# First weights on ScalarE's queue, rounded by VectorE; x, the norm's factors and y in one tile; the first step product by product

## The chip, the cores and the metric

The kernel runs on one core of one Trainium2 chip. The metric is the device time of one execution in microseconds. The time before is the median of three executions, 852.4 us (852.05 to 853.03).

A core has a matrix engine (TensorE, PE in the profile, its weight loads PEld), a vector engine (VectorE, DVE), a scalar engine (ScalarE, ACT), a third elementwise engine (GpSimd, POOL) and an engine that only issues transfers here (SyncE, SP). SP and ACT can both issue transfers (SPq and ACTq in the profile). PE accumulates into PSUM banks; ACT, DVE and POOL work on SBUF tiles of 128 partitions.

## The reference

Two encoder layers over 512 tokens of 1024 features. Each layer is RMS norm, one wide input projection, a local attention, a SiLU gate, an output projection and a residual sum:

```python
def rms_norm(x, g):
    xf = x.astype(jnp.float32)
    y = xf * lax.rsqrt(jnp.mean(xf * xf, axis=-1, keepdims=True) + RMS_EPS)
    return (y * g.astype(jnp.float32)).astype(x.dtype)

def mixer_a(hn, w_in, w_out, q_gain, k_gain, t5_bias):
    proj = hn @ w_in                       # 1024 x (9 * 1024 + 1024)
    for g, (window, dilation) in enumerate(DILATED_PAIRS):
        q = rms_norm(qkv[:, :, g, 0], q_gain[g])
        k = rms_norm(qkv[:, :, g, 1], k_gain[g])
        o, lse = dilated_group_attention(q, k, qkv[:, :, g, 2], ...)
        ...
    y = jnp.sum(alpha[..., None] * jnp.stack(outs), axis=0)
    return (y.reshape(b, s, BRANCH_WIDTH) * jax.nn.silu(gate)) @ w_out

def reference(x, norm_gain, ...):
    for i in range(DEPTH):                 # DEPTH = 2
        hn = rms_norm(x, norm_gain[i])
        y = mixer_a(hn, ...) if i % 2 == 0 else mixer_b(hn, ...)
        x = x + y
    return x
```

The second mixer has the same form with attention on an 8 x 64 grid of tokens. Everything is float32.

## The kernel before, in words

**Products.** The matrix engine takes float32 operands in a rounded form (F32R). To keep float32 precision each operand is split in a rounded part h and the rest l, and each product is made of three matmuls into one bank: h by h, h by l, l by h (`mm3`). Weights are loaded as plain float32 (`wraw`), and `split` makes `wh` (rounding copy on ScalarE, line 127) and `wl` (the difference, line 131, on VectorE or, for two of five, on GpSimd). The same is done with the normed input: `norm` makes `hn_h` (ScalarE, line 379) and `hn_l` (VectorE, line 380) from x and the norm's factors `ng`. The row scale of the norm is not in `hn`; it is multiplied in after the projection.

**Steps.** A projection (`project`) adds over eight steps k of 128 features. In each step four blocks of 128 tokens get one product (three matmuls) each, so a step is twelve matmuls of 128 x 512. The order on PE is the order of the program; the instructions of the other engines are placed by a scheduler with a model of time, except those under `keep_in_program_order`, which stay where they stand. A second thread of the program (`side`) emits norms, squares and attention between the matmuls: after each block of matmuls the main thread lets it go on as far as a modelled clock says.

**Streams.** `raws` loads the weights in the order of use, two steps in one tile of 1024 columns (`wraw`, three buffers), all on SP's queue. The first tile is loaded in two halves, with x's second slice between them. `splits` works up to four steps ahead (four buffers of `wh` and `wl`).

**The start.** SP issues x's first slice (128 x 512), the first weights (128 x 512), x's second slice, the second weights, and then larger pieces of x and weights in turn. ScalarE's queue issues `ng` (128 x 16) and `hg` (128 x 8, the head gains). VectorE makes four products `gk` of `hg` (line 366); first use is much later, in `k_a`. Meanwhile PE runs nine matmuls on ones (`busy`, line 358) whose result is not used. Then step 0 begins. `side` squares each slice of x in place once it is normed (`square_a`), adds the slices up (line 1146) and gets the row scale.

**y.** x's first copy `x_all` (16 KB per partition) has the tag "y"; when it is no longer read, `y_h` takes its place. `y_l` is a tile of its own. Both are written once per head pair (`put_y`) and read by the output projections (`out_product`).

Of the kernel before, what the change touches and what calls it, by code (L numbers as in the profile page):

```python
# [13 lines left out]
F32 = mybir.dt.float32  # L14
F32R = mybir.dt.float32r
I32 = mybir.dt.int32
AF = mybir.ActivationFunctionType
ALU = mybir.AluOpType
# [4 lines left out]
P = 128  # L23
S = 512
# [3 lines left out]
KT = 8  # L28
EPS = 1e-6
SCALE = DH ** -0.5  # L30
# [12 lines left out]
def tile_hybrid_encoder(  # L43
# [2 lines left out]
    xt: bass.AP,  # L46
    xg: bass.AP,
    w: bass.AP,
    norm_gain: bass.AP,
    head_gain: bass.AP,  # L50
    t5t: bass.AP,
    rpb: bass.AP,
# [4 lines left out]
    nc = tc.nc  # L57
# [3 lines left out]
    big = ctx.enter_context(tc.tile_pool(name="big", bufs=1))  # L61
# [21 lines left out]
    def bank(name):  # L83

        return ps_side.tile([P, 512], F32, tag="side", name=name)
# [13 lines left out]

    hn_h = big.tile([P, KT, S], F32R, name="hn_h")  # L100
    hn_l = big.tile([P, KT, S], F32R, name="hn_l")
    x_all = big.tile([P, KT, S], F32, tag="y", name="x_all")
    y_l = big.tile([P, KT, S], F32R, name="y_l")

    def rsqrt(eng, r, ss, n, scale):
        v = wk.tile([P, 32], F32, tag="nv", name="nv", bufs=1)
# [15 lines left out]
    turn, pool = [0], [2, 5]  # L122

    def split(raw, n):
        h = wp.tile([P, 512], F32R, tag="wh", name="wh", bufs=4)[:, :n]
        l = wp.tile([P, 512], F32R, tag="wl", name="wl", bufs=4)[:, :n]
        nc.scalar.copy(h, raw)  # L127
        turn[0] += 1
        to_pool = turn[0] * pool[0] % pool[1] < pool[0]
        eng = nc.gpsimd if to_pool else nc.vector  # L130
        eng.tensor_sub(l, raw, h.bitcast(F32))  # L131
        return h, l
# [24 lines left out]
    def loads():  # L157
        for off, n, ks in blocks():
            per = 1024 // n
            for k in range(0, ks, per):  # L160
                m = min(per, ks - k)
                yield w[:, off + k * n : off + (k + m) * n], m * n, n
# [3 lines left out]
    def raws():  # L166
        queue = []
        for src, cols, n in loads():
            raw = wp.tile([P, 1024], F32, tag="wraw", name="wraw", bufs=3)
            dst = raw[:, :cols]  # L170
            if not begun:
                nc.sync.dma_start(dst[:, :n], src[:, :n])
                begun.append(load_x(1, 2))
                dst, src = dst[:, n:], src[:, n:]
            nc.sync.dma_start(dst, src)
            if behind:
                behind.pop()()
            queue.append((raw, cols, n))
            if len(queue) > 2:
                yield queue.pop(0)  # L180
        yield from queue
# [30 lines left out]
    def mm3(o, lh, ll, rh, rl, first, last):  # L212
        matmul(o, lh, rh, start=first, stop=False)
        matmul(o, lh, rl, start=False, stop=False)
        matmul(o, ll, rh, start=False, stop=last)
# [26 lines left out]
    def project(stat_h, stat_l, n, evac, guard, need=None):  # L242

        acc = {i: ps_acc.tile([P, 512], F32, tag="acc", name="acc") for i in range(4)}
        for k in range(KT):
            chore(1 <= k < KT - 2)
            if need:
                yield need, min(k + 1, KT - 1)
            if k == KT - 1:
                yield guard  # L250
            h, l = next(wsteps)
            for i in range(4):
                mm3(acc[i][:, :n], stat_h(k, i), stat_l(k, i), h, l, k == 0, k == KT - 1)
                if k == KT - 1:
                    evac(i, acc[i])
                yield
# [69 lines left out]
    ng = cp.tile([P, 2, KT], F32, name="ng")  # L326
# [13 lines left out]
        rsqrt(nc.vector, rs_n, ssq, 4, 1.0 / D)  # L340

    def load_x(k0, k1):
        nc.sync.dma_start(x_all[:, k0:k1, :], xt[:, k0:k1, :])

    warm = cp.tile([P, 1], F32, name="warm")
    nc.vector.memset(warm, 0.0)
    nc.scalar.activation(warm, warm, AF.Exp)
    load_x(0, 1)
    nc.scalar.dma_start(ng, norm_gain)
    behind += [  # L350
        lambda: load_x(6, KT),
        lambda: load_x(4, 6),
        lambda: load_x(2, 4),
    ]
    busy = bank("busy")
    for _ in range(9):
        wide = lambda n: ones[:, 0:1].to_broadcast([P, n])
        nc.tensor.matmul(busy, wide(P), wide(S), start=True, stop=True)
    wsteps = steps()
    wsteps = chain([next(wsteps)], wsteps)  # L360

    hg = cp.tile([P, 8], F32, name="hg")
    nc.scalar.dma_start(hg, head_gain)
    gk = cp.tile([P, 4], F32, name="gk")
    for i, (a, b) in enumerate(((0, 3), (1, 4), (2, 5), (6, 7))):
        nc.vector.scalar_tensor_tensor(
            gk[:, i : i + 1], hg[:, a : a + 1], -SCALE, hg[:, b : b + 1], op0=ALU.mult, op1=ALU.mult
        )

    def scales_a():  # L370
        pa = spread()
# [2 lines left out]

    def norm(layer, k, xk):

        g = ng[:, layer, k : k + 1]
        h, l = hn_h[:, k, :], hn_l[:, k, :]
        nc.scalar.activation(h, xk, AF.Copy, scale=g)
        return nc.vector.scalar_tensor_tensor(l, xk, g, h.bitcast(F32), op0=ALU.mult, op1=ALU.subtract)  # L380
# [38 lines left out]
    st = {}  # L419
# [237 lines left out]
    def put_y(hc, o, permuted, last):  # L657

        gt, rest = st.pop(("gate", hc))
        for _ in rest:  # L660
            pass
        if last and permuted:
            for c in range(4):
                q = slice(P * c, P * c + P)
                of = lambda t: t.rearrange("p (s x) -> p s x", x=16)[:, :, 4 * c : 4 * c + 4]
                nc.vector.tensor_mul(of(gt), of(gt), of(o))
                src = gt.rearrange("p (t ja x) -> p x ja t", t=4, ja=8)[:, 4 * c : 4 * c + 4]
                h, l = (t[:, hc, q].rearrange("p (x ja t) -> p x ja t", x=4, ja=8) for t in (st["y_h"], y_l))
                nc.scalar.copy(h, src)
                nc.vector.tensor_sub(l, src, h.bitcast(F32))  # L670
            return
        h, l, src = st["y_h"][:, hc, :], y_l[:, hc, :], gt
        if permuted:

            tc.keep_in_program_order(nc.vector.tensor_mul(gt, gt, o))
            src = gt.rearrange("p (t ja x) -> p x ja t", t=4, ja=8)
            h, l = (t.rearrange("p (x ja t) -> p x ja t", t=4, ja=8) for t in (h, l))
        else:
            for grid, line in ((mid_rc, mid_o), (edge_rc, edge_o)):
                nc.vector.tensor_mul(grid(gt), grid(gt), line(o))  # L680
        nc.scalar.copy(h, src)
        (nc.vector if last else nc.gpsimd).tensor_sub(l, src, h.bitcast(F32))
        stamp["ya" if permuted else "yb", hc, "y"] = 0
# [239 lines left out]
    def out_product(key, sink):  # L923


        acc = {}

        def step(k, tiles):
            h, l = next(wsteps)
            for i, f in enumerate(tiles):  # L930
                c = slice(P * i, P * i + P)
                mm3(acc[f], h[:, c], l[:, c], st["y_h"][:, k, :], y_l[:, k, :], k == 0, k == KT - 1)
                if k == KT - 1:
                    sink(f, acc[f])
                yield

        for f in range(4):
            acc[f] = ps_acc.tile([P, 512], F32, tag="acc", name="acc")
        for k in range(KT - 1):
            chore(True)  # L940
            yield key, k, "y"
            yield from step(k, range(4))
        yield key, "turned"
        for f in range(4, 7):
            acc[f] = bank("acc2")
        for k in range(KT - 1):
            yield from step(k, range(4, 7))
        yield key, KT - 1, "y"
        yield from step(KT - 1, range(4))
        yield from step(KT - 1, range(4, 7))  # L950
        acc[7] = ps_acc.tile([P, 512], F32, tag="acc", name="acc")
        for k in range(KT):
            yield from step(k, (7,))
# [182 lines left out]
    def side():  # L1136
        for k in range(KT):
            norm(0, k, x_all[:, k, :])
            if k:
                square_a(k - 1)  # L1140
            stamp["na", k] = 0
            yield 1000
        square_a(KT - 1)
        for k in range(1, KT):
# [1 line left out]
            nc.vector.tensor_add(x_all[:, 0, :], x_all[:, 0, :], x_all[:, k, :])  # L1146
        yield 1500
        row_scale(row_sums(x_all[:, 0, :]))
        st["y_h"] = big.tile([P, KT, S], F32R, tag="y", name="y_h")
        yield 2500  # L1150
        bias_lines()
        st["e", 0] = bias_a(0)
# [64 lines left out]
def _layout(x, norm_gain, a_w_in, a_w_out, a_q_gain, a_k_gain, t5_bias,  # L1217
            b_w_in, b_w_out, b_q_gain, b_k_gain, b_rpb):
    f = lambda a: np.asarray(a)
    x, norm_gain, t5_bias = f(x), f(norm_gain), f(t5_bias)  # L1220
# [13 lines left out]
    for hc in range(NHC):  # L1234
        c = lambda g, i: (3 * g + i) * D + P * hc
# [9 lines left out]
    w = np.concatenate(parts, axis=1)  # L1245

    hg = np.concatenate([f(a_q_gain)[0], f(a_k_gain)[0], f(b_q_gain), f(b_k_gain)]).T
    hg = np.concatenate([hg, hg])
    rt = f(b_rpb)[0].transpose(0, 2, 1)
    rpb = np.stack([rt[:, :, 7 - r + _GRID_ROWS] for r in _GRID_ROWS], axis=1).reshape(P, 248)  # L1250
    oh, mask = _constants()
    norm_gain = norm_gain.reshape(2, KT, P).transpose(2, 0, 1)
    xt = x[0].reshape(P, 4, KT, P).transpose(3, 2, 1, 0).reshape(P, KT, S)
    xg = x[0].reshape(8, 64, KT, P)[_GRID_ROWS].transpose(3, 2, 1, 0).reshape(P, KT, S)
    return [xt, xg, w, norm_gain, hg, t5_bias.T, rpb, oh, mask]


_NAMES = ["xt", "xg", "w", "norm_gain", "head_gain", "t5t", "rpb", "onehot", "maskc"]


# [17 lines left out]
```

## Time and profile before

| | before |
|---|---|
| median of the runs | 852.4 us |
| the profiled execution's own time | 854.65 us |
| span of that execution in the profile | 852.7 us |
| TensorE busy | 843.6 us (99%) |
| VectorE, ScalarE, GpSimd busy | 520.2, 431.3, 307.1 us |
| transfers | 141.23 MB, mean 166 GB/s |

The span runs from the first to the last instruction; the execution's own time is longer by what lies around it. A row of the timeline gives the start and the duration in us, the engine, the line of the kernel, the operation, what is written from what, the shape, and in brackets how long the engine had been idle before and what ended that. Matmuls are pipelined and their ends are modelled, so the distance of two starts says more of PE's pace than a duration. A row of the waits gives engine, line and tile, what it waited for, and us in total, number, longest. In a row of windows stand the window, its length, the busy time and number of instructions of PE, PEld, DVE, ACT and POOL, the granted clock, the DMA engines' busy share, and GB/s.

### The profile page before, as it was taken

What the parts mean: (1) busy time and instruction counts of PE and PEld (TensorE: products, weight loads), DVE (VectorE), ACT (ScalarE), POOL (GpSimd) and SP (SyncE); (2) the same over time, 40 slices, a digit from 0 to 9 for tenths busy, and PEclk for the clock granted to TensorE, in tenths of its full rate; (3) what the DMA queues carried; (4) which work ended last, traced back from release to release, by engine and by line L of the source; (5) the groups of instructions that cost most, each with busy time, mean ns of one, the idle gap of its engine ahead of it and who ended that gap; (6) DMA issues with size and microseconds to landing.
All of it is one profiled execution on the core that took longest, in us unless ns stands there. A gap on an engine that the chain in (4) does not pass through costs nothing.

```text
span 852.7 us, 15400 instructions
## 1 busy us (share of the span) xinstructions
PE 843.6 (99%) x5547; PEld 702.7 (82%) x5547; DVE 520.2 (61%) x1335; ACT 431.3 (51%) x924; POOL 307.1 (36%) x493
## 2 busy tenths in 40 slices
PE   8999999999999999999999999999999999999998
PEld 6788878788788788788788787789998898889786
DVE  6445684674675675675675745447567656766642
ACT  7433653653652652652653554355366655665531
POOL 2252541542542542542531341121344335542411
PEclk9999999999999999999999999999999999999999
DMA  7346277477478378378375562174245654555223
GB/s 250 111 130 208 87 226 219 153 222 227 137 230 241 105 239 240 98 238 238 96 247 153 147 190 78 60 244 142 82 142 150 168 162 149 170 163 160 99 98 126
DMA packets 65372, 141.23 MB, mean 166 GB/s; under 512 B 5904, under 2 KB 23248, under 8 KB 65296
## 3 DMA queue, kind: packets, MB, share of 16 engines
q1 hardware_dynamic: 65008, 140.24, 53.7%
q8 instruction: 44, 0.72, 0.4%
q14 instruction: 32, 0.26, 0.1%
q10 hardware_dynamic: 288, 0.01, 0.0%
HBM read 109.11 MB, written 31.12 MB: 164 GB/s over the span
## 4 chain that ended last, share of the span: by engine, by line
PE 87%; ACT 4%; DMA 4%; DVE 3%; issue 1%; POOL 1%; SPq 0%; ACTq 0%; POOLq 0%; DVEq 0%
PE acc L206 74%; PE log L206 5%; PE o L206 5%; PE tp L210 3%; DMA qd<-rawq 1%; ACT p L655 1%; ACT p L814 1%; DMA rp<-in_rpb 1%; ACT p L1067 1%; DMA qt<-qd 1%; POOL sq L270 1%; ACT wh L127 1%; DMA hg<-in_head_gain 0%; DVE wl L131 0%; DMA eb<-lb_d 0%
## 5 line engine op out<-in xcount | busy, mean ns | idle before, releaser
L127 ACT CAST wh<-wraw 128x512 fp32r<-128x512 f32 (+1 forms) x276 | 162.0, 588 | 291.4 <-PE acc L206 251.0
L206 PE MATMUL acc<-wh,hn_h 128*128 128x512 f32 (+1 forms) x768 | 294.2, 383 | 1.7 <-ACT wh L127 0.9
L206 PE MATMUL acc<-wh,hn_l 128*128 128x512 f32 (+1 forms) x768 | 286.3, 373 | 0.0
L206 PE MATMUL acc<-wl,hn_h 128*128 128x512 f32 (+1 forms) x768 | 285.8, 372 | 0.4 <-DVE wl L131 0.4
L131 POOL TENSOR_TENSOR wl<-wraw,wh 128x512 fp32r<-128x512 f32 (+1 forms) x110 | 137.0, 1245 | 359.4 <-ACT wh L127 320.0
L131 DVE TENSOR_TENSOR wl<-wraw,wh 128x512 fp32r<-128x512 f32 (+1 forms) x166 | 111.1, 670 | 135.8 <-ACT wh L127 131.5
L206 PEld LDWEIGHTS acc<-wh,hn_h 128*128 128x128 f32 x768 | 144.6, 188 | 29.3 <-issue 4.9
L206 PEld LDWEIGHTS acc<-wh,hn_l 128*128 128x128 f32 x768 | 144.4, 188 | 20.8
L206 PEld LDWEIGHTS acc<-wl,hn_h 128*128 128x128 f32 x768 | 144.8, 189 | 19.8 <-DVE wl L131 0.9
L206 PE MATMUL acc<-hn_h,wh 128*128 128x512 f32 x192 | 77.0, 401 | 0.9 <-ACT rawq L460 0.6
L206 PE MATMUL acc<-hn_h,wl 128*128 128x512 f32 x192 | 74.9, 390 | 0.0
L206 PE MATMUL acc<-hn_l,wh 128*128 128x512 f32 x192 | 74.8, 390 | 0.0
L655 ACT ACTIVATE p<-p,mn 128x512 f32<-128x512 f32 (+3 forms) x128 | 69.3, 586 | 0.0
L814 ACT ACTIVATE p<-p,mn 128x512 f32<-128x512 f32 (+1 forms) x64 | 44.8, 701 | 45.0 <-DVE mn L803 44.1
L273 DVE TENSOR_REDUCE ss<-sq 128x4 f32<-128x256 f32 (+1 forms) x96 | 48.4, 504 | 30.7 <-POOL sq L272 19.7
L727 DVE STREAM_TRANSPOSE tr<-p 128x512 f32<-128x512 f32 (+1 forms) x80 | 53.7, 682 | 9.9 <-ACT p L655 9.5
L272 POOL TENSOR_TENSOR sq<-rawk 128x256 f32<-128x256 f32 x64 | 40.5, 639 | 52.7 <-ACT rawk L460 44.9
L206 PE MATMUL acc<-y_h,wh 128*128 128x512 f32 x128 | 52.1, 407 | 0.0
L206 PE MATMUL acc<-y_h,wl 128*128 128x512 f32 x128 | 50.0, 391 | 0.0
L206 PE MATMUL acc<-y_l,wh 128*128 128x512 f32 x128 | 49.9, 390 | 0.0
L206 PEld LDWEIGHTS acc<-hn_h,wh 128*128 128x128 f32 x192 | 36.1, 188 | 10.8 <-ACT rawk L460 2.1
L206 PEld LDWEIGHTS acc<-hn_h,wl 128*128 128x128 f32 x192 | 36.0, 188 | 7.7
(138 smaller groups left out, 1087.0 us busy)
## 6 DMA issues: line engine op xcount, KB each, us to landing
wraw<-in_w SPq DMA_DIRECT2D x95, 512.0 KB
wraw<-in_w SPq DMA_DIRECT2D x38, 384.0 KB
td<-tr SPq DMA_DIRECT2D x14, 1024.0 KB
pt<-td SPq DMA_DIRECT2D x56, 256.0 KB
qd<-rawq SPq DMA_DIRECT2D x6, 1024.0 KB
qt<-qd SPq DMA_DIRECT2D x24, 256.0 KB
td<-tr SPq DMA_DIRECT2D x6, 896.0 KB
pt<-td SPq DMA_DIRECT2D x24, 224.0 KB
```

Source lines behind the costliest of these rows:

```text
L127: nc.scalar.copy(h, raw)
L131: eng.tensor_sub(l, raw, h.bitcast(F32))
L206: nc.tensor.matmul(o, l, r, **kw)
L210: nc.tensor.transpose(o, i, ident)
L270: nc.gpsimd.tensor_mul(sq.rearrange("p (f a r) -> p a f r", f=4, a=4), v, v)
L272: nc.gpsimd.tensor_mul(sq, v, v)
L273: nc.vector.tensor_reduce(ss[:, i * ns : (i + 1) * ns], sq.rearrange("p (a b) -> p a b", b=64), axis=AX.X, op=ALU.add)
L655: nc.scalar.activation(pr, pr, AF.Copy, scale=mn[:, 3:4])
L727: nc.vector.transpose(dst, src[:, :n].rearrange("p (i b k) -> p i b k", b=4, k=32))
L814: nc.scalar.activation(row, row, AF.Exp, bias=mn[:, 1:2], scale=-1.0, accum_out=mn[:, 2:3])
L1067: nc.scalar.activation(pr[:, o : o + n], pr[:, o : o + n], AF.Exp, bias=mn[:, 0:1], scale=-1.0, accum_out=mn[:, 2:3])
```

## The change

- The first half tile of weights is issued by ScalarE in place of SP. `ng` has no transfer of its own: its 16 columns stand in front of x in memory, and come with x's first slice into one tile. `hg` is issued on SP's queue, and it and `gk` are emitted when the norm of k = 4 has been emitted, `gk` in program order. For the second layer GpSimd copies the factors out of the tile.
- The first weights are rounded by VectorE in place of ScalarE; all later ones by ScalarE as before.
- In step 0 of the first projection the twelve matmuls go product by product: four of h by h, four of h by l, four of l by h, and the side thread is let in once after them, not after each block.
- Eight matmuls on ones in place of nine.
- `y_h` and `y_l` are halves of one tile of 32 KB per partition, in the place of the tile that x and the factors had.

The diff, without the lines that only pass names on:

```diff
+    x_ng = big.tile([P, 2 * KT * S], F32, tag="y", name="x_all")[:, : 2 * KT + KT * S]
+    x_all = x_ng[:, 2 * KT :].rearrange("p (k t) -> p k t", k=KT)
...
     def split(raw, n):
-        nc.scalar.copy(h, raw)
+        if turn[0]:
+            nc.scalar.copy(h, raw)
+        else:
+            nc.vector.tensor_copy(h, raw)
         turn[0] += 1
...
             if not begun:
-                nc.sync.dma_start(dst[:, :n], src[:, :n])
+                nc.scalar.dma_start(dst[:, :n], src[:, :n])
                 begun.append(load_x(1, 2))
...
             h, l = next(wsteps)
+            if need and k == 0:
+                for i in range(4):
+                    matmul(acc[i][:, :n], stat_h(k, i), h, start=True, stop=False)
+                for i in range(4):
+                    matmul(acc[i][:, :n], stat_h(k, i), l, start=False, stop=False)
+                for i in range(4):
+                    matmul(acc[i][:, :n], stat_l(k, i), h, start=False, stop=False)
+                yield
+                continue
...
     def load_x(k0, k1):
-        nc.sync.dma_start(x_all[:, k0:k1, :], xt[:, k0:k1, :])
+        lo = 2 * KT + S * k0 if k0 else 0
+        hi = 2 * KT + S * k1
+        nc.sync.dma_start(x_ng[:, lo:hi], xt[:, lo:hi])
...
     load_x(0, 1)
-    nc.scalar.dma_start(ng, norm_gain)
...
-    for _ in range(9):
+    for _ in range(8):
...
-    nc.scalar.dma_start(hg, head_gain)
     gk = cp.tile([P, 4], F32, name="gk")
-    for i, (a, b) in enumerate(((0, 3), (1, 4), (2, 5), (6, 7))):
-        nc.vector.scalar_tensor_tensor(
-            gk[:, i : i + 1], hg[:, a : a + 1], -SCALE, hg[:, b : b + 1], op0=ALU.mult, op1=ALU.mult
-        )
+    def gains():
+        nc.sync.dma_start(hg, head_gain)
+        nc.gpsimd.tensor_copy(ng.rearrange("p l k -> p (l k)"), x_ng[:, : 2 * KT])
+        for i, (a, b) in enumerate(((0, 3), (1, 4), (2, 5), (6, 7))):
+            m = nc.vector.scalar_tensor_tensor(
+                gk[:, i : i + 1], hg[:, a : a + 1], -SCALE, hg[:, b : b + 1], op0=ALU.mult, op1=ALU.mult
+            )
+            tc.keep_in_program_order(m)
...
     def norm(layer, k, xk):
-        g = ng[:, layer, k : k + 1]
+        g = (ng if layer else x_ng[:, : 2 * KT].rearrange("p (l k) -> p l k", l=2))[:, layer, k : k + 1]
...
             stamp["na", k] = 0
+            if k == 4:
+                gains()
             yield 1000
...
-        st["y_h"] = big.tile([P, KT, S], F32R, tag="y", name="y_h")
+        y = big.tile([P, 2 * KT * S], F32R, tag="y", name="y").rearrange("p (n k t) -> p n k t", n=2, k=KT)
+        st["y_h"], st["y_l"] = y[:, 0], y[:, 1]
```

More of the change, by code (lines that the diff above doesn't have):

```diff
@@ L48, in tile_hybrid_encoder @@
     w: bass.AP,
-    norm_gain: bass.AP,
     head_gain: bass.AP,
@@ L101, in tile_hybrid_encoder @@
     hn_l = big.tile([P, KT, S], F32R, name="hn_l")
-    x_all = big.tile([P, KT, S], F32, tag="y", name="x_all")
-    y_l = big.tile([P, KT, S], F32R, name="y_l")
+    x_ng = big.tile([P, 2 * KT * S], F32, tag="y", name="x_all")[:, : 2 * KT + KT * S]
+    x_all = x_ng[:, 2 * KT :].rearrange("p (k t) -> p k t", k=KT)
     def rsqrt(eng, r, ss, n, scale):
@@ L667, in put_y @@
                 src = gt.rearrange("p (t ja x) -> p x ja t", t=4, ja=8)[:, 4 * c : 4 * c + 4]
-                h, l = (t[:, hc, q].rearrange("p (x ja t) -> p x ja t", x=4, ja=8) for t in (st["y_h"], y_l))
+                h, l = (t[:, hc, q].rearrange("p (x ja t) -> p x ja t", x=4, ja=8) for t in (st["y_h"], st["y_l"]))
                 nc.scalar.copy(h, src)
@@ L671, in put_y @@
             return
-        h, l, src = st["y_h"][:, hc, :], y_l[:, hc, :], gt
+        h, l, src = st["y_h"][:, hc, :], st["y_l"][:, hc, :], gt
         if permuted:
@@ L931, in step @@
                 c = slice(P * i, P * i + P)
-                mm3(acc[f], h[:, c], l[:, c], st["y_h"][:, k, :], y_l[:, k, :], k == 0, k == KT - 1)
+                mm3(acc[f], h[:, c], l[:, c], st["y_h"][:, k, :], st["y_l"][:, k, :], k == 0, k == KT - 1)
                 if k == KT - 1:
@@ L1251, in _layout @@
     oh, mask = _constants()
-    norm_gain = norm_gain.reshape(2, KT, P).transpose(2, 0, 1)
-    xt = x[0].reshape(P, 4, KT, P).transpose(3, 2, 1, 0).reshape(P, KT, S)
+    norm_gain = norm_gain.reshape(2, KT, P).transpose(2, 0, 1).reshape(P, 2 * KT)
+    xt = x[0].reshape(P, 4, KT, P).transpose(3, 2, 1, 0).reshape(P, KT * S)
+    xt = np.concatenate([norm_gain, xt], axis=1)
     xg = x[0].reshape(8, 64, KT, P)[_GRID_ROWS].transpose(3, 2, 1, 0).reshape(P, KT, S)
-    return [xt, xg, w, norm_gain, hg, t5_bias.T, rpb, oh, mask]
-_NAMES = ["xt", "xg", "w", "norm_gain", "head_gain", "t5t", "rpb", "onehot", "maskc"]
+    return [xt, xg, w, hg, t5_bias.T, rpb, oh, mask]
+_NAMES = ["xt", "xg", "w", "head_gain", "t5t", "rpb", "onehot", "maskc"]
 def kernel(**inputs):
```

## The prediction, on record before the result

> **What bounds the kernel now.** I read the page first, then the timelines of the first 30 us engine by engine, because every edit but the shared tile for y lies there.
>
> ```profile
> span 852.7 us, 15400 instructions
> PE 843.6 (99%) x5547; PEld 702.7 (82%) x5547; DVE 520.2 (61%) x1335; ACT 431.3 (51%) x924; POOL 307.1 (36%) x493
> ```
>
> PE is idle for 852.7 - 843.6 = 9.1 us in all, so only PE's own idle time, or slow PE time, can be won. The list of what PE waited for shows where:
>
> ```profile
> PE acc L206 <- ACT rawq L460: 1.4, 2, 0.8
> PE o L206 <- DMA eb<-lb_d: 0.9, 1, 0.9
> PE busy L358 <- DVE warm L346: 0.9, 1, 0.9
> PE acc L206 <- ACT wh L127: 0.9, 1, 0.9
> PE acc L206 <- DVE wl L131: 0.4, 1, 0.4
> PE tp L210 <- ACT p L655: 0.4, 1, 0.4
> ```
>
> Three of these waits (0.9 for the first filler matmul, 0.9 for the first wh, 0.4 for the first wl) are at the start. PE's timeline there (columns: start, duration, instruction):
>
> ```profile
> 0.92 4.21 PE L358 MATMUL busy<-ones 128*128 128x512 f32 x9 [0.92 <-DVE warm L346]
> 6.00 0.80 PE L206 MATMUL acc<-wh,hn_h 128*128 128x512 f32 x1 [0.88 <-ACT wh L127]
> 7.20 0.80 PE L206 MATMUL acc<-wl,hn_h 128*128 128x512 f32 x1 [0.40 <-DVE wl L131]
> 7.79 0.63 PE L206 MATMUL acc<-wh,hn_l 128*128 128x512 f32 x1
> 8.22 0.63 PE L206 MATMUL acc<-wh,hn_h 128*128 128x512 f32 x1
> 9.50 0.58 PE L206 MATMUL acc<-wh,hn_h 128*128 128x512 f32 x1
> 9.92 0.40 PE L206 MATMUL acc<-wl,hn_h 128*128 128x512 f32 x1
> 10.16 0.39 PE L206 MATMUL acc<-wh,hn_l 128*128 128x512 f32 x1
> 10.39 0.40 PE L206 MATMUL acc<-wh,hn_h 128*128 128x512 f32 x1
> 11.08 0.39 PE L206 MATMUL acc<-wh,hn_h 128*128 128x512 f32 x1
> 13.83 0.39 PE L206 MATMUL acc<-wh,hn_h 128*128 128x512 f32 x1
> 14.05 0.39 PE L206 MATMUL acc<-wl,hn_h 128*128 128x512 f32 x1
> 22.44 0.39 PE L206 MATMUL acc<-wh,hn_l 128*128 128x512 f32 x1
> ```
>
> Step 0 (k = 0, twelve matmuls) runs from 6.00 to 11.08. Matmuls stand 0.43 us apart until 9.92 (7.79 to 8.22), and 0.23 us apart after it (10.16 to 10.39). So PE runs at half speed up to 9.9 us, although the page prints a granted clock of full speed. From 11.08 on a step takes 2.75 us (to 13.83) without a gap. The waits left in the list (on rawq, eb and p) are on tiles that the first projection doesn't have, so they come later.
>
> What feeds step 0, from the timelines of ScalarE, VectorE and the two queues:
>
> ```profile
> 0.74 0.38 SPq L343 DMA_DIRECT2D x_all<-in_xt  x1
> 1.18 0.41 SPq L172 DMA_DIRECT2D wraw<-in_w  x1
> 0.73 0.40 ACTq L349 DMA_DIRECT2D ng<-in_norm_gain  x1
> 1.23 0.39 ACTq L363 DMA_DIRECT2D hg<-in_head_gain  x1
> 3.66 0.72 ACT L379 ACTIVATE hn_h<-x_all,ng 128x512 fp32r<-128x512 f32 x1 [0.99 <-DMA ng<-in_norm_gain]
> 5.33 0.62 ACT L127 CAST wh<-wraw 128x512 fp32r<-128x512 f32 x1 [0.95 <-DMA wraw<-in_w]
> 5.51 0.37 DVE L366 SCALAR_TENSOR_TENSOR gk<-hg 128x1 f32<-128x1 f32 x4 [4.61 <-DMA hg<-in_head_gain]
> 5.80 0.75 DVE L380 SCALAR_TENSOR_TENSOR hn_l<-x_all,ng,hn_h 128x512 fp32r<-128x512 f32 x1
> 6.46 0.69 DVE L131 TENSOR_TENSOR wl<-wraw,wh 128x512 fp32r<-128x512 f32 x1
> ```
>
> The chain is: weights land 5.33, rounded 5.95, PE starts 6.00. VectorE sits until 5.51 for hg, does gk, then hn_l, then wl at 6.46, so PE's second matmul starts at 7.20.
>
> **The change part by part.**
>
> *First weights issued by ScalarE.* The issue moves from 1.18 (third in time) to the slot at 0.73 that ng leaves: 0.45 us earlier. The later SP issues move up by the same 0.45, but the transfers can't all follow, since the DMA engines are busy already:
>
> ```profile
> 2.00:3.00 1.00, 1.00 (x4) 0.82 (x3) 0.00 (x0) 0.65 (x2) 0.00 (x0) 1.00 0.90 284
> 6.00:7.00 1.00, 0.80 (x1) 0.29 (x1) 1.00 (x2) 0.42 (x1) 0.00 (x0) 1.00 1.02 387
> ```
>
> (the last two columns are DMA busy share and GB/s). The weights' landing is bounded by 0.73 + (3.66 - 0.74) = 3.65 below, if they take the time that x needed ahead of them, and by today's 5.33 above. The nearest row is hg: 128 x 8 floats (4 KB) issued on ScalarE's queue at 1.23 were there only at 5.51, as late as the 128 x 512 floats (256 KB) issued on SP at 1.18. So two queues share the engines, and a transfer on ScalarE's queue does not overtake. I take 5.33 - 0.45 = 4.88 for the weights, and the same for x, which now shares with them instead of going first (3.66 to 5.33). [...]
>
> *The factors in x's tile.* One transfer in place of two; 64 bytes more on rows of 2048, 3% of a transfer. ng no longer can be the late one; x itself is. Nothing gained, under 0.05 us lost. The 8 and 4 KB transfers leave ScalarE's queue, which costs nothing there.
>
> *First rounding on VectorE.* ScalarE's first hn_h (0.72) and the rounding (0.62 on ScalarE) no longer queue behind each other. A VectorE copy of this shape isn't in the trace from SBUF; between zero and the two-input 0.69 above I take 0.69. Then hn_h is ready at 4.88 + 0.72 = 5.60, wh at 5.57, and with 0.05 to PE the first matmul starts at 5.65. Gain 0.35; bounds: 3.65 + 0.72 + 0.05 = 4.42 (gain 1.58) and 5.33 + 0.72 + 0.05 = 6.10 (loss 0.10).
>
> *Product by product.* The first four matmuls need only wh and hn_h. At 0.43 us the fifth, which needs wl, comes at 5.65 + 1.72 = 7.37; the ninth, which needs hn_l, at 9.09. On VectorE wh ends 5.57, wl 6.26, hn_l 7.01; even at 0.23 us per matmul they'd be due at 6.57 and 7.49. So the hole between 6.00 and 7.20 closes: 1.20 - 0.43 = 0.77, and 0.16 of the next spacing (7.79 - 7.20 - 0.43). Step 0 is emitted as one block, so norms of later k come about half a step later in program order; the supply rows below have that to spare.
>
> *Eight fillers for nine.* PE is free 0.43 earlier, at 4.70; it idles then to 5.65 (0.95 against 0.88). Free of cost unless the clock depends on it (below).
>
> *gk moved behind k = 4, hg on SP's queue, and a POOL copy of ng.* VectorE loses a 4.61 us wait. gk (0.37) returns later, in VectorE's queue behind hn_l of k = 4, with hn_l and wl of later steps queued behind it; POOL has not begun its first wl then or idles between them. Costed at nothing where hg has landed by then; if not, see the third rival.
>
> *y_h and y_l in one tile.* No instruction more. x's last reader and the first writer of y_l are far apart:
>
> ```profile
> L682 POOL TENSOR_TENSOR y_l<-gt,y_h x14: 1287/1438/1586, 159.6 to 802.8; 128x512 fp32r<-128x512 f32 x14
> 34.23 0.95 PE L206 MATMUL pk<-ones,x_all 128*128 128x1 f32 x8
> ```
>
> **What is late next.** The next steps need their weights (rows of VectorE, POOL, ScalarE):
>
> ```profile
> 8.52 0.69 DVE L131 TENSOR_TENSOR wl<-wraw,wh 128x512 fp32r<-128x512 f32 x1
> 11.09 1.40 POOL L131 TENSOR_TENSOR wl<-wraw,wh 128x512 fp32r<-128x512 f32 x1 [9.66 <-ACT wh L127]
> 10.40 1.13 ACT L127 CAST wh<-wraw 128x512 fp32r<-128x512 f32 x2
> ```
>
> Step 1's wl is there at 9.21, used at 11.31: 2.1 us to spare. Step 2's comes from POOL at 12.49 and is used at 14.05: 1.56 to spare. So PE can come 1.56 us earlier with no change in the supply. Beyond that, step 2 holds it, unless its supply comes earlier too. ScalarE loses 0.62 us of work and the wait for the late hn_l, so 0.5 to 0.9 earlier is likely; the cap on the gain is 2.1 to 2.5.
>
> **Sum.** 0.35 + 0.77 + 0.16 = 1.28 us, if the clock rises after as many slow matmuls as before. Then step 1 begins at 9.80, step 2 at 12.55, its wl is due at 12.78 against 12.49. From there PE has no gap until the later waits of the list, and weight loads follow PE's release of buffers, so the gain is kept. The profiled execution took 854.65 us around its span of 852.7, 2.25 us above the median of 852.4; its time would become 853.4, the span 851.4, and the median 852.4 - 1.3 = 851.1.
>
> **The rivals.**
>
> *The clock rises at the same time, not after the same work (chance 0.17).* Then ten matmuls from 5.65 to 9.92 are slow, two quick: step 1 begins at 10.38, gain 0.7, time 851.7. For it: in both kernels PE idles about 0.9 us just before step 0. Against: the hole at 6.4 to 7.2 is gone. [...]
>
> *The clock rises early, during or right behind the fillers (0.25).* Then step 0 takes 12 x 0.23 = 2.8 us from 5.65, step 1 begins at 8.4, and step 2's supply is the limit: gain 2.1 to 2.5, time 850.1. For it: no hole within step 0. Against: nine fillers with 0.88 idle behind them didn't do it here, and now there are eight with 0.95.
>
> *hg comes late (slower, 0.08).* SP issues in order, and its loads wait for weight buffers:
>
> ```profile
> 5.88 0.43 SPq L397 DMA_DIRECT2D t<-in_t5t  x1
> 9.24 13.41 SPq L175 DMA_DIRECT2D wraw<-in_w  x4
> 14.36 2.45 DVE L380 SCALAR_TENSOR_TENSOR hn_l<-x_all,ng,hn_h 128x512 fp32r<-128x512 f32 x2
> ```
>
> If hg is queued behind these four, it is issued at 22.65 and there at 22.65 + 4.28 = 26.9. gk holds VectorE, so hn_l of k = 5 is done at 27.7 where PE wants it at 22.44 - 1.28 = 21.2: a wait of 6.5, net 5.2 slower, 857.6. It decides once hg lands after about 20.4. Against it: t5's small load, which stands far behind these in the program (L397), was issued at 5.88, ahead of the four.
>
> *The transfers share so that neither is earlier (0.13).* x lands at 5.33, first matmul 6.10; only the hole closes, partly at the fixed time of the clock's rise: gain 0 to 0.8, 852.0.
>
> **How the numbers follow.** The forecast has 0.34, the rivals 0.17, 0.25, 0.08, 0.13; 0.03 is left for shifts in the four later waits of PE (0.4 to 0.9 us each). About 0.2%, 1.7 us, is what a measurement of this kernel can tell from no change. Faster by more: the early clock and a quarter of the forecast, 0.33. Slower by more: late hg and a little of the rest, 0.11. Within: 0.56. The range goes from 849.6 (cap of 2.5 and a later wait of 0.3 gone) to 853.4 (loss of 0.1 at the start and one later wait of 0.9 more).
>
> **What would show it.** Right: ScalarE's queue issues the weights at about 0.7, first wh on VectorE, first matmul near 5.65, no gap within step 0, step 1 at about 9.8. Wrong: a first matmul before 5 or after 6, spacings of 0.23 before 7 us, a PE wait in steps 1 to 5 on wl or hn_l, VectorE waiting for hg, or later PE waits that differ by over 1 us together.

## The result, and the profile after

The changed kernel took 851.91 us (median of 22 runs, 850.25 to 853.14) against 852.37 us for the kernel before (22 runs, 851.72 to 853.97). The ratio is 0.9985, with a 95% interval of 0.9979 to 0.9991: 1.3 us (0.8 to 1.8) faster. The prediction was 1.3 us.

The medians alone differ by only 0.46 us, and why is most of this section's lesson. The runs of each kernel fall in two groups:

| | lower group | mean | upper group | mean |
|---|---|---|---|---|
| before | 12 runs, 851.72 to 852.40 | 852.03 | 10 runs, 853.03 to 853.97 | 853.50 |
| after | 10 runs, 850.25 to 851.50 | 850.72 | 12 runs, 851.88 to 853.14 | 852.46 |

Within the groups the change gains 1.31 and 1.04 us; the mean over all runs goes from 852.70 to 851.67, by 1.03. So the gain is 1.0 to 1.3 us by every measure but the medians of all runs. The median of 22 falls into the lower group before and next to the border of the upper one after. The profiled execution of after took 852.44 us (span 850.6), so it is one of the upper group, and that of before (854.65) lies above its upper group.

The page of after:

```profile
span 850.6 us, 15397 instructions
PE 842.8 (99%) x5546; PEld 702.5 (83%) x5546; DVE 518.5 (61%) x1336; ACT 431.5 (51%) x923; POOL 309.8 (36%) x494
```

Of the 2.1 us between the spans 0.8 is PE's busy time (843.6 to 842.8, one filler and the slow matmuls) and 1.3 its idle time (9.1 to 7.8). What PE waited for, after (us in total, times, longest):

```profile
PE acc L209 <- ACT rawq L477: 1.4, 2, 0.8
PE busy L371 <- DVE warm L360: 0.9, 1, 0.9
PE acc L209 <- ACT hn_h L396: 0.7, 1, 0.7
PE tp L213 <- ACT p L672: 0.4, 1, 0.4
PE o L209 <- DMA eb<-lb_d: 0.2, 1, 0.2
```

The waits on the first wh (0.9) and wl (0.4) are gone, one on hn_h (0.7) has come. The other 0.7 us of idle time that went is the late wait on eb, which no part of the change touches; in the profiles of the experiments it is at most 0.8 and in two of them not listed at all, so it is scatter between executions. The start, in the timelines of PE, ScalarE, VectorE, GpSimd and SP of after:

```profile
0.92 3.78 PE L371 MATMUL busy<-ones 128*128 128x512 f32 x8 [0.92 <-DVE warm L360]
5.41 2.07 PE L209 MATMUL acc<-wh,hn_h 128*128 128x512 f32 x4 [0.71 <-ACT hn_h L396]
7.28 1.91 PE L209 MATMUL acc<-wl,hn_h 128*128 128x512 f32 x4
8.98 1.39 PE L209 MATMUL acc<-wh,hn_l 128*128 128x512 f32 x4
10.21 0.39 PE L209 MATMUL acc<-wh,hn_h 128*128 128x512 f32 x1
0.73 0.41 ACTq L175 DMA_DIRECT2D wraw<-in_w  x1
4.63 1.38 ACT L396 ACTIVATE hn_h<-x_all 128x512 fp32r<-128x512 f32 x2 [1.96 <-DMA x_all<-in_xt]
4.81 0.43 DVE L130 CAST wh<-wraw 128x512 fp32r<-128x512 f32 x1 [3.91 <-DMA wraw<-in_w]
5.27 0.69 DVE L134 TENSOR_TENSOR wl<-wraw,wh 128x512 fp32r<-128x512 f32 x1
5.88 1.41 DVE L397 SCALAR_TENSOR_TENSOR hn_l<-x_all,hn_h 128x512 fp32r<-128x512 f32 x2
15.81 0.36 DVE L382 SCALAR_TENSOR_TENSOR gk<-hg 128x1 f32<-128x1 f32 x4
10.24 1.33 POOL L134 TENSOR_TENSOR wl<-wraw,wh 128x512 fp32r<-128x512 f32 x1 [5.38 <-ACT wh L128]
5.17 0.65 SPq L379 DMA_DIRECT2D hg<-in_head_gain  x1
```

Step 0 starts at 5.41 in place of 6.00, runs its three products without a gap, and step 1 starts at 10.21 in place of 11.08. So 0.87 us are gained by step 1: 0.59 by the earlier start, and only 0.28 by a shorter step 0 (4.80 in place of 5.08). PE keeps the slow pace through the second product: the four starts from 7.28 to 8.98 are 0.43 us apart. The third product takes 8.98 to 10.21, 1.23 us for four, so the clock rises in it, somewhat earlier than the 9.92 of before. "The clock rises" stands, here and below, for the change of the spacing from 0.43 to 0.23 us ("half speed" for 0.43). That a clock is behind it is the author's reading: the column for the granted clock has 1.00 at both spacings, in every microsecond from 0 to 13 of before and of after.

### The profile page after: what moved, and what is told of

It is laid out like the page before. It is cut to its first block, busy times and chain, and to the rows that moved or that the text cites. A ratio compares the mean times of both kernels' runs of the same rounds, so it can differ in the third digit from the quotient of the medians.

```text
span 850.6 us, 15397 instructions
## 1 busy us (share of the span) xinstructions
PE 842.8 (99%) x5546; PEld 702.5 (83%) x5546; DVE 518.5 (61%) x1336; ACT 431.5 (51%) x923; POOL 309.8 (36%) x494
## 4 chain that ended last, share of the span: by engine, by line
PE 94%; ACT 3%; DVE 1%; DMA 1%; issue 0%; DVEq 0%; ACTq 0%
PE acc L209 80%; PE log L209 5%; PE o L209 5%; PE tp L213 3%; ACT p L1084 1%; ACT p L672 1%; DMA x_all<-in_xt 0%; ACT p L831 0%; ACT wh L128 0%; DVE hn_l L397 0%; ACT rawk L477 0%; DMA eb<-lb_d 0%; PE pa L209 0%; PE pl L209 0%; DVE p L820 0%
## 5 line engine op out<-in xcount | busy, mean ns | idle before, releaser
L209 PE MATMUL acc<-y,wh 128*128 128x512 f32 x256 | 81.3, 399 | 0.0
L209 PEld LDWEIGHTS acc<-y,wh 128*128 128x128 f32 x256 | 46.3, 188 | 10.2 <-issue 1.1
L209 PE MATMUL acc<-y,wl 128*128 128x512 f32 x128 | 50.0, 391 | 0.0
```

The source lines that it names most:

```text
L209: nc.tensor.matmul(o, l, r, **kw)
```

## The experiments

The theory: the two groups are early and late rises of PE's clock, and what lies between the fillers and step 0 decides which. The rival: the groups come from when x and the weights land. In the table, "step 0" and "step 1" are the starts read from the profiled execution's PE timeline; the times are those of all runs.

| run | fillers | median, us | lowest to highest | runs | step 0 | step 1 | profiled, us |
|---|---|---|---|---|---|---|---|
| after, ten fillers | 10 | 850.96 | 850.80 to 851.24 | 5 | 5.35 | 8.55 | 850.96 |
| after, four fillers | 4 | 853.42 | 851.83 to 855.18 | 11 | 5.52 | 10.81 | 853.79 |
| after, block by block | 8 | 852.64 | 851.10 to 853.78 | 11 | 5.32 | 10.25 | 852.83 |
| after, weights on SP | 8 | 853.15 | 851.56 to 854.31 | 11 | 5.69 | 8.81 | 851.56 |
| after, eleven fillers | 11 | 850.95 | 850.51 to 851.40 | 10 | 5.34 | 8.19 | 851.18 |
| eleven, ScalarE rounds | 11 | 851.58 | 851.16 to 852.37 | 11 | 6.16 | 9.01 | 851.81 |
| eleven, block by block | 11 | 851.51 | 851.35 to 852.07 | 11 | 5.77 | 9.23 | 852.06 |
| eleven, weights on SP | 11 | 851.61 | 850.81 to 853.00 | 11 | 5.45 | 9.05 | 852.53 |
| after again | 8 | 852.23 | 850.73 to 853.33 | 12 | 5.16 | 7.98 | 851.02 |
| before, eleven fillers | 11 | 851.88 | 851.55 to 852.51 | 11 | 6.27 | 10.11 | 852.51 |
| eleven, hg early | 11 | 851.29 | 850.44 to 852.31 | 11 | 5.78 | 8.83 | 851.29 |
| after, ten again | 10 | 850.68 | 850.29 to 851.38 | 10 | 5.44 | 8.89 | 851.14 |

Each four rows ran on one chip, and the kernel before had medians of 854.00, 853.63 and 853.14 on these three.

**Ten and four fillers.**

```diff
-    for _ in range(8):
+    for _ in range(10):        # and range(4) in the other
```

> The changed kernel with ten filler matmuls in place of eight. The runs of both kernels fall in two groups: before 851.7 to 852.4 and 853.0 to 854.0, after 850.2 to 851.5 and 851.9 to 853.1. Theory (clock): the groups are early and late rises of PE's clock, and the hole between the fillers and step 0 decides which. Ten fillers end at 0.92 + 10 x 0.43 = 5.2, 0.2 before step 0 at 5.4, so nearly every run falls in the early group: median 850.6, ratio about 0.998, spacing of 0.23 us before 7.8 us in the profile. Rival (loads): the groups come from when x and the weights land, PE only waits for them; then ten fillers change nothing and the runs still fall in two groups around 850.7 and 852.4.

> The changed kernel with four fillers: they end at 0.92 + 4 x 0.43 = 2.6 and PE idles 2.8 us before step 0 at 5.4. Theory (clock): the early rise is never had, all runs are in the late group or above it, 852.2 to 853.2, no run under 851.6, and in the profile the spacing is 0.43 until 8.8 to 12. Rival (loads): two groups as before, 850.7 and 852.4.

Ten fillers: all five runs lie within 0.44 us, 850.96 in the median, ratio to before 0.9967 (0.9955 to 0.9980). PE's timeline:

```profile
0.92 4.63 PE L371 MATMUL busy<-ones 128*128 128x512 f32 x10 [0.92 <-DVE warm L360]
5.35 1.54 PE L209 MATMUL acc<-wh,hn_h 128*128 128x512 f32 x4
6.72 1.08 PE L209 MATMUL acc<-wl,hn_h 128*128 128x512 f32 x4
7.64 1.07 PE L209 MATMUL acc<-wh,hn_l 128*128 128x512 f32 x4
8.55 0.39 PE L209 MATMUL acc<-wh,hn_h 128*128 128x512 f32 x1
```

The second and third products have starts 0.23 us apart (6.72 to 7.64 for four); the clock rises in the first product. The operands came hardly earlier than in after (step 0 at 5.35 against 5.41). That is the theory's reading, and against the loads.

Four fillers went the other way in the profile: the whole of step 0 is slow.

```profile
0.92 2.08 PE L371 MATMUL busy<-ones 128*128 128x512 f32 x4 [0.92 <-DVE warm L360]
5.52 2.08 PE L209 MATMUL acc<-wh,hn_h 128*128 128x512 f32 x4 [2.53 <-ACT hn_h L396]
7.40 1.91 PE L209 MATMUL acc<-wl,hn_h 128*128 128x512 f32 x4
9.10 1.91 PE L209 MATMUL acc<-wh,hn_l 128*128 128x512 f32 x4
10.81 0.61 PE L209 MATMUL acc<-wh,hn_h 128*128 128x512 f32 x1
```

The median of 853.42 is above the forecast band, and no run is as low as with ten. But the runs still spread, four from 851.83 to 852.36 and seven from 853.20 to 855.18, where the theory had one late group. So some moment varies between executions there as well. No lower run of four fillers was profiled, so what varies there stays open.

**Block by block, and the weights on SP, with eight fillers.**

```diff
-            if need and k == 0:
-                for i in range(4):
-                    matmul(acc[i][:, :n], stat_h(k, i), h, start=True, stop=False)
...
-                yield
-                continue
```

```diff
-                nc.scalar.dma_start(dst[:, :n], src[:, :n])
+                nc.sync.dma_start(dst[:, :n], src[:, :n])
```

> The changed kernel with step 0 block by block again (h h, h l, l h of one block, then the next). Theory (sum of the prediction): the second matmul waits for wl, which ends at 5.96 in the profile of after, and the third for hn_l at 6.6, against starts of 5.84 and 6.27: a wait of about 0.1 and 0.3, so only 0.2 to 0.5 us of the gain is due to the order, since wl now follows closely: median 852.2. Rival: the hole of 1.2 us comes back whole and the order carries 0.8 to 0.9 us: median 852.8.

> The changed kernel with the first weights issued on SP's queue again. Theory (the queues share the engines): x lands first again, at 3.7 to 4.0 in place of 4.6, the weights at 4.9 to 5.3; with the rounding of 0.43 on VectorE step 0 starts at 5.3 to 5.8, within 0.4 us of after: median within 0.4 us of after. Rival (the issue on ScalarE is what brings the start forward): step 0 starts at 5.9 to 6.0 and the time rises by 0.5 us or more.

With eight fillers both runs spread over 2.7 us, so their medians (852.64 and 853.15) tell little of a part worth half a microsecond, and after itself was not on that chip. Their profiles do tell: block by block, step 0 starts as in after, with small holes; with the weights on SP it starts at 5.69, within the 5.3 to 5.8 of the first theory.

**Eleven fillers as a base.** With the groups gone, the parts can be weighed.

> The changed kernel with eleven fillers, as the base for the next three: with ten, all five runs lay within 0.5 us, so the parts can be told apart without the two groups. Theory (clock): one narrow group again; at half speed the eleven end at 0.92 + 11 x 0.43 = 5.65, up to 0.25 after the operands of step 0, but the clock then rises earlier: 850.7 to 851.4, 0.0 to 0.3 above ten fillers. Rival (loads): two groups 1.5 us apart.

The runs lie in 850.51 to 851.40, median 850.95, ratio to before 0.9973 (0.9964 to 0.9982). PE's timeline:

```profile
0.92 4.58 PE L371 MATMUL busy<-ones 128*128 128x512 f32 x11 [0.92 <-DVE warm L360]
5.34 1.20 PE L209 MATMUL acc<-wh,hn_h 128*128 128x512 f32 x4
```

Here the clock rises within the fillers: eleven at 0.43 us would have kept PE until about 5.8, as in two profiles below. On this base each of three parts was undone:

```diff
-        if turn[0]:
-            nc.scalar.copy(h, raw)
-        else:
-            nc.vector.tensor_copy(h, raw)
+        nc.scalar.copy(h, raw)
```

> Eleven fillers, and the first weights rounded on ScalarE as before the change. Theory (the two ScalarE jobs queue): x and the weights now land within 0.2 us of each other (4.6 and 4.8), so the rounding (0.62) comes behind hn_h (0.72) on ScalarE, step 0 starts 0.5 to 0.6 us later, at 5.9 to 6.0, and with the fillers' end at 5.65 some 0.3 us reaches the end: 0.3 to 0.6 us above eleven fillers. Rival (nothing): the fillers hide it all: within 0.15 us.

> Eleven fillers, and step 0 block by block. Theory: wl ends at 5.9 and hn_l at 6.5 while the first matmul starts at 5.4 to 5.65, so the second and third wait 0.1 to 0.5 us together: 0.1 to 0.5 us above eleven fillers; step 2's wl at 12.1 is the next limit and takes part of that away. Rival: the hole of 1.2 us comes back whole: 0.8 us or more above.

> Eleven fillers, and the first weights on SP's queue. With eight fillers step 0 started at 5.69 in place of 5.41 and x's second slice landed at 6.5 in place of 5.4, so hn_h of k = 1 and all that follows on ScalarE came 1.2 us later, and PE waited for step 2's wl until 12.17. Theory (supply): that cap costs more than the start: 0.8 to 1.5 us above eleven fillers, with a PE wait at step 2. Rival (start only): 0.0 to 0.3 us above, since the start moves by 0.28 and eleven fillers cover that.

(The edits of the second and third are the two diffs above.)

*ScalarE rounds: 851.58, 0.63 slower.* The timeline of ScalarE and PE:

```profile
4.87 0.62 ACT L127 CAST wh<-wraw 128x512 fp32r<-128x512 f32 x1 [2.19 <-DMA wraw<-in_w]
5.39 1.33 ACT L393 ACTIVATE hn_h<-x_all 128x512 fp32r<-128x512 f32 x2
...
6.16 1.20 PE L206 MATMUL acc<-wh,hn_h 128*128 128x512 f32 x4 [0.29 <-ACT hn_h L393]
```

The two jobs queue on ScalarE in the other order than expected (rounding first), with the same effect: step 0 at 6.16 in place of 5.34, with 0.29 of idle time. That is the expected mechanism, just above its price of 0.3 to 0.6.

*Block by block: 851.51, 0.56 slower.* The waits are where they were expected:

```profile
5.77 0.56 PE L209 MATMUL acc<-wh,hn_h 128*128 128x512 f32 x1
6.17 0.49 PE L209 MATMUL acc<-wl,hn_h 128*128 128x512 f32 x1
6.83 0.50 PE L209 MATMUL acc<-wh,hn_l 128*128 128x512 f32 x1 [0.17 <-DVE hn_l L388]
7.17 0.39 PE L209 MATMUL acc<-wh,hn_h 128*128 128x512 f32 x1
```

The second matmul comes 0.40 after the first, the third 0.66 after it, the fourth 0.34: against 0.23 these are 0.17, 0.43 and 0.11, 0.7 us together, against 0.56 in the medians. The start of step 0 at 5.77 in place of 5.34 is not the order's doing: in this execution all eleven fillers ran at half speed (5.06 us, against 4.58 on the base). It took 852.06, 0.55 above the median.

*Weights on SP: 851.61, 0.66 slower*, between the two expectations, with the supply theory's mechanism. (Its runs spread over 2.2 us, and the profiled one took 852.53.) Here the load of x's second slice is third in SP's queue, behind the first weights:

```profile
3.50 0.72 ACT L396 ACTIVATE hn_h<-x_all 128x512 fp32r<-128x512 f32 x1 [1.27 <-DMA x_all<-in_xt]
7.24 0.72 ACT L396 ACTIVATE hn_h<-x_all 128x512 fp32r<-128x512 f32 x1 [3.03 <-DMA x_all<-in_xt]
...
9.05 0.51 PE L209 MATMUL acc<-wh,hn_h 128*128 128x512 f32 x1 [0.32 <-ACT wh L128]
9.78 0.50 PE L209 MATMUL acc<-wl,hn_h 128*128 128x512 f32 x1 [0.22 <-DVE wl L134]
...
12.40 0.39 PE L209 MATMUL acc<-wh,hn_h 128*128 128x512 f32 x1
12.86 0.50 PE L209 MATMUL acc<-wl,hn_h 128*128 128x512 f32 x1
```

x's first slice is there at 3.50, a microsecond earlier than in after, and the second at 7.24. In after ScalarE makes both slices in one go from 4.63 (two in 1.38 us), so the second had landed by about 5.3: almost two microseconds earlier. Step 0 starts at 5.45, but step 1 now waits for its wh and wl, and step 2 for its wl (12.86, 0.46 after the matmul ahead of it at 12.40). So what the issue on ScalarE's queue is worth lies in what no longer stands behind the first weights on SP, not in the first weights.

The three prices, 1.85 us together, are more than what the change is worth without the clock's scatter (0.9 to 1.2 us, below). So the parts overlap, and each price holds only with the other parts in place.

**After again, before with eleven fillers, hg early, ten again.**

```diff
-    for _ in range(9):          # the kernel before
+    for _ in range(11):
```

```diff
+    nc.scalar.dma_start(hg, head_gain)
     gk = cp.tile([P, 4], F32, name="gk")
+    for i, (a, b) in enumerate(((0, 3), (1, 4), (2, 5), (6, 7))):
+        nc.vector.scalar_tensor_tensor(
+            gk[:, i : i + 1], hg[:, a : a + 1], -SCALE, hg[:, b : b + 1], op0=ALU.mult, op1=ALU.mult
+        )
...
-        nc.sync.dma_start(hg, head_gain)        # and the four of gk, in gains()
```

> The changed kernel itself, as the neighbour of the next three on one chip. Theory (clock): its runs spread over both groups (from 850.2 to 853.2), 1 us and more wider than with ten or eleven fillers, and its median lies 0.5 to 1.5 us above theirs. Rival (chip): on this chip it lies as closely together as they do.

> The kernel before with eleven fillers in place of nine and nothing else. Theory (clock): the fillers end at 5.65, PE idles 0.35 before step 0 at 6.0, and the upper group of its runs (853.0 and more) goes: all runs in 851.7 to 852.4, median 852.0. What is left between that and eleven fillers on the changed kernel (850.95) is what the rest of the change is worth: about 1.1 us. Rival (the hole within step 0, 0.8 us, spoils the clock anyway): two groups as before, median 853 or more.

> The changed kernel with eleven fillers, hg's load on ScalarE's queue at the start and gk where the scheduler wants it, as before the change. Theory (not on the path): gk comes behind wl on VectorE, hn_l 0.4 us later, and it isn't needed until the third product: within 0.2 us of eleven fillers. Rival (small rows slow the first transfers: in the profile of before 224 GB/s from 3 to 4 us with hg under way, after it 353): x and the weights land 0.3 to 0.6 later, and the time rises by 0.3 to 0.6.

> Ten fillers once more, beside the changed kernel on the same chip. Theory (clock): one group, 850.7 to 851.3. Rival: its five runs of the first time were lucky, and some now lie at 852 or more.

*After again* has five runs from 850.73 to 851.35 and seven from 852.20 to 853.33, and this time a lower one was profiled (851.02, span 849.2). It is the same program as the upper one above; PE's timeline:

```profile
5.16 1.18 PE L209 MATMUL acc<-wh,hn_h 128*128 128x512 f32 x4 [0.46 <-ACT hn_h L396]
6.17 1.07 PE L209 MATMUL acc<-wl,hn_h 128*128 128x512 f32 x4
7.08 1.07 PE L209 MATMUL acc<-wh,hn_l 128*128 128x512 f32 x4
7.98 0.39 PE L209 MATMUL acc<-wh,hn_h 128*128 128x512 f32 x1
...
10.70 0.39 PE L209 MATMUL acc<-wh,hn_h 128*128 128x512 f32 x1
11.15 0.50 PE L209 MATMUL acc<-wl,hn_h 128*128 128x512 f32 x1
```

Step 0 begins 0.25 earlier than in the upper one, but takes 2.82 us in place of 4.80: the clock rises at its beginning. So the two groups are two moments of the clock in one program, seen in a trace of each. The loads also came 0.25 earlier here (hn_h at 4.38 in place of 4.63), but that is only the 0.25 of the start. The other profiles with four to nine fillers fit: where the spacing of 0.43 lasts beyond 9.3 us (before, four fillers, block by block) the execution took 852.8 us or more, and with the weights on SP, where it has ended when step 0 begins, 851.56. The groups are not always clean, though: of the 34 runs of the kernel before on this chip six lie between 852.6 and 853.2. Step 1 starts 2.23 us earlier and the span is 1.4 shorter; 0.2 of the difference goes at once into step 2's second product (11.15 - 10.70 = 0.45 in place of 0.23), the cap that the prediction put there.

*Ten again*: 850.29 to 851.38 in ten runs beside it, ratio to before 0.9972 (0.9963 to 0.9982). Fifteen runs of ten fillers on two chips, none above 851.4, against nineteen of thirty-four of after above 851.5.

*Before with eleven fillers*: 851.55 to 852.51, median 851.88; the upper group is gone here too, although the hole within step 0 stayed. PE's timeline there:

```profile
6.27 0.50 PE L206 MATMUL acc<-wh,hn_h 128*128 128x512 f32 x1 [0.53 <-ACT wh L127]
7.49 0.50 PE L206 MATMUL acc<-wl,hn_h 128*128 128x512 f32 x1 [0.71 <-DVE wl L131]
7.82 0.40 PE L206 MATMUL acc<-wh,hn_l 128*128 128x512 f32 x1
```

The first matmul takes 0.50 us here and took 0.80 in the profile of before (with modelled ends), and the distance from the second to the third is 0.33 in place of 0.59. So the clock has risen by then, and the hole doesn't bring the slow pace back. In this execution PE also idles for 0.53 us ahead of step 0, about as long as in after again (0.46); it is the slowest of the eleven, and still below the upper group. So the gap alone doesn't decide; eleven fillers also keep PE busy longer than nine (4.83 us here, 4.21 in before). Whether the length of the fillers or the gap behind them matters was not separated.

By the means of all runs on this chip the two more fillers are worth 1.1 us (853.05 to 851.93), by the recorded ratio, 0.9991 (0.9982 to 0.9999), 0.8. The distance to ten fillers on the changed kernel, 1.2 us (851.88 - 850.68), is what the rest of the change is worth without the clock's scatter. Against eleven fillers there (850.95, on another chip) it is 0.9, where 1.1 was expected.

*hg early*: 851.29, 0.34 above eleven fillers on another chip and 0.61 above ten on this one, within the bounds of neither theory clearly. In its profile x and the weights land as in after (ScalarE's hn_h at 4.60, VectorE's rounding at 4.77), gk stands behind wl and hn_l begins at 6.12, and PE has no wait for it. So the rival's mechanism isn't in the trace. What the trace does show is that step 0 starts at 5.78, 0.44 later than on the base of eleven, because here all eleven fillers ran at half speed:

```profile
0.92 5.06 PE L371 MATMUL busy<-ones 128*128 128x512 f32 x11 [0.92 <-DVE warm L360]
5.78 1.38 PE L209 MATMUL acc<-wh,hn_h 128*128 128x512 f32 x4
```

That would fit 0.3 to 0.6 with no part for hg, but it is one execution, and the cause is not settled.

## Why the prediction was right, step by step

**The size.** 1.28 us was forecast and 1.3 (0.8 to 1.8) measured, 1.31 and 1.04 within the groups. The forecast of 851.1 us was taken from one median of three runs, 852.4, which lay in the lower group, and the measured median of 851.91 in the upper one; this, not the gain, makes the difference of 0.8.

That 1.28 comes so near to 1.3 is in part luck. In the two profiled executions, one of each kernel and both with a late rise, step 1 came forward from 11.08 to 10.21, by 0.87, and not to the 9.80 of the forecast:

| | forecast, us | in the profiles, us |
|---|---|---|
| step 0 starts earlier | 0.35 | 0.59 |
| the hole within step 0 | 0.93 | 0.77 |
| the clock, in step 0 | 0 | -0.49 |
| step 1 starts earlier | 1.28 | 0.87 |

The third row is what remains. The 0.16 that the hole lacks is the longer first distance behind an idle gap: in before it was 7.20 to 7.79, 0.59, and in after it is there again, 5.41 to 6.00. The sum's condition, that the clock rises after as many slow matmuls as before, did not hold: seven distances in step 0 were at the slow pace before, between nine and ten after, and the clock rose at about 9.6 us against 9.9. That is nearer to the rival "at the same time" (step 1 at 10.38) than to the forecast. For the lower groups, 1.31 us apart, no profile of the kernel before was taken.

**The landing.** Predicted: both at 4.88, x later and the weights earlier. Measured 4.63 and 4.81. The reading of hg's row, that a transfer on ScalarE's queue shares the engines and doesn't overtake, held for the first weights: issued on ScalarE's queue at 0.73, they are first used 0.18 after x (issued on SP's at 0.74), and x itself comes later than in before (4.63 against 3.66); with the weights on SP x is there at 3.50 (eleven fillers; 3.42 with eight). Not seen was another effect: x's second slice, which no longer stands behind the first weights on SP, is used by about 5.3, where with the weights on SP it landed at 7.24 (eleven fillers; 6.55 with eight). The prediction said that the later transfers "can't all follow"; by that comparison this one did. (In the kernel before, the slice was first used at 7.12, behind other work of ScalarE, so when it landed there isn't shown.) Step 2's wl came 0.85 earlier (10.24 against 11.09), at the upper end of the 0.5 to 0.9 that was put down to ScalarE's lighter load. With eleven fillers it came at 9.72, and at 11.35 with the weights on SP, which points to the place of x's second slice in the queue for much of that.

**The rounding on VectorE.** Taken as 0.69, the time of the two-input operation in the profile of before; measured 0.43, the same in all eleven profiles in which VectorE does it. Why one input takes less than two, no run shows. Of the 0.26 us saved 0.14 counted: hn_h (4.63 + 0.73 = 5.36) came last, and at 0.69 wh would have been ready at 5.50. Step 0 started at 5.41 in place of the 5.65 forecast because x landed 0.25 earlier and wh was ready by then.

**The hole in step 0.** Closed, as forecast. But the order by products is not alone in that: undone on the base of eleven fillers it costs 0.56. The rest of the hole is put down to VectorE's wait for hg, which in the kernel before held hn_l and wl until 5.80 and 6.46; after, wl starts at 5.27. No run tested that by itself.

**gk and hg.** hg was issued at 5.17, ahead of the four loads that wait for buffers, and gk ran at 15.81 in VectorE's stream without a wait. The slower rival did not happen, for the reason given against it.

**The clock.** Here the prediction was right in its alternatives and wrong in treating them as one answer. "After the same work", "at the same time" and "early" were three rivals with a chance each, but the changed kernel has both early and late rises in different executions, ten of its 22 runs being in the lower group. For the kernel before, with twelve of 22 there, this is inferred from the groups, since no lower run of it was profiled. The argument "nine fillers with 0.88 idle behind them didn't do it here" came from one execution, an upper one; by the groups, in other runs they did. One filler less with the start 0.6 earlier left the share of early rises about as it was.

**The later waits.** They were left out of the sum, rightly: eb's wait is 0.9 in the profile of before and between 0.8 and nothing listed in the others, with no relation to the edits.

**A better version.** Ten fillers on the changed kernel beat both: 0.9967 (0.9955 to 0.9980) and 0.9972 (0.9963 to 0.9982) of before, on two chips, against 0.9985 and 0.9988 (0.9979 to 0.9996) for the change itself. Eight fillers leave PE idle for 0.46 to 0.71 us ahead of step 0, and the time at which PE is free earlier is of no use. Nine on the changed kernel were not tried.

## What to carry to other kernels

Where PE is the bound and its first matmuls are slow (here 0.43 us apart, later 0.23), lay enough filler matmuls that they reach the first real one: here two more fillers were worth as much as all the rest of the change (1.1 us by the means, on either kernel, against 1.2), and with eight or nine fillers and a gap behind them the time was a matter of luck. Look at all runs of a kernel before taking a median as its time; when they fall in groups, compare within groups, or remove the cause first and then weigh the parts on that base. When a transfer is moved to another queue, look at what stood behind it in the old one: here that, x's second slice, is what arrived earlier (used by about 5.3, against 7.24 with the weights on SP and eleven fillers).

## What the runs showed of the hardware

- PE's matmuls of 128x512 start 0.43 us apart at first and 0.23 us apart later, and the moment of the change differs between executions of one program: in the two profiles of after step 0 takes 4.80 and 2.82 us. Of the fourteen profiles ten have the change before 7.1 us and three between 9.3 and 9.9; in that of four fillers the starts are still 0.43 us apart up to 10.81. The column for the granted clock doesn't show it (1.00 in every microsecond from 0 to 13, before and after); only the distance of the starts tells. What sets the moment, no run here shows. Nine fillers (4.21 us in before, the end modelled) with 0.88 us of idle time behind them in the profile left ten of the 22 runs of before in the upper group; of 25 runs of after with ten or eleven, which reach to the first real matmul, none was.
- x's first slice and the first weights (264 and 256 KB), issued at 0.74 and 0.73 with a queue each, are first used within 0.2 us of each other (4.63 and 4.81, after), and 1.4 apart on one queue (3.50 and 4.87, weights on SP with eleven fillers).
